# A gated recurrence whose projections take seven block products for eight (one Trainium2 core)

## The chip, the cores and the metric

The kernel runs on one core of a Trainium2 chip. The metric is the device time of one execution in microseconds (us); of several executions the median is taken. The engines have short names: PE (TensorE, matrix products), DVE (VectorE), ACT (ScalarE), POOL (GpSimd) and SP (SyncE, which here only issues DMAs). Each takes its instructions strictly in the order in which they were laid, and waits at an instruction until what it needs is there.

## The reference

A decoder trunk of two layers on 1024 tokens of width 1024, in float32. Layer 0 mixes tokens by a gated linear recurrence (HGRN2), layer 1 by sliding-window attention; each is followed by a gated convolution FFN of width 2816. The change touches the mixer of layer 0:

```python
def hgrn2_mixer(h, w_in, lower_bound, g_norm_w, w_out):
    q, f, i, g = jnp.split(h @ w_in, 4, axis=-1)          # 8 heads of 128 each
    lb = lower_bound.reshape(HG_HEADS, HG_DIM)
    fg = lb + (1.0 - lb) * jax.nn.sigmoid(heads(f))
    o = hgrn2_chunkwise(jax.nn.silu(heads(q)), 1.0 - fg, heads(i), jnp.log(fg))
    o = o * lax.rsqrt(jnp.mean(jnp.square(o), -1, keepdims=True) + RMS_EPS)
    o = o * g_norm_w * jax.nn.silu(heads(g))
    return o.reshape(B, S, D) @ w_out
```

So each head needs four projections of the 1024 x 1024 input x: q (query), f (forget gate), i (values) and g (output gate), each with a 1024 x 128 block of the weights. Then come the recurrence itself, a normalisation by 1/rms, the gate, and the output projection `w_out`.

## The kernel before

Everything is one program on one core, laid by a Python generator. `Order` keeps two clocks while it lays instructions: `od.t`, an estimate of TensorE's time, which every matmul moves on, and `od.v`, an estimate of DVE's. Tasks are generators that say how long to wait on `od.t`; `od.tick`, called after each few matmuls, lays what is due. `od.fill` lays small DVE jobs where DVE's clock is behind. So the order on all engines is written out by hand, and the engines follow it whatever the true times are.

A float32 product is made of three matmuls in a rounded format, "high" times "high", "high" times "low", "low" times "high" (`mm3`, L193 to L197): an operand is split into a rounded copy, written by ACT, and the rest, written by DVE (`low_part`, L166). The input x is turned once, so that features lie on partitions, and lies split in `T`; split weights pass through the twelve places of `HL`, raw weights through three `raw` tiles loaded by SP.

Per head h:

- `qf` (L915) projects f and q, feature-major: 2 halves of 512 tokens x 8 blocks of 128 features x `mm3` each. ACT forms the gate by Sigmoid and two affine steps; q times its sigmoid is formed on DVE (L934).
- `ig_block` (L726) projects i and g token-major: for each of 8 blocks of 128 tokens, 8 pairs of a 512-column and a 256-column matmul (L738, L739). `values` (L698) adds the two halves of the result and forms g times its sigmoid.
- `recur` (L944) is the recurrence of one head: DVE steps by powers of two (`update`), many small matmuls into `psax`, the state `St`, and the output. It is laid into the projections of the next head, so that TensorE has other work while it waits for DVE. `norm` (L1115) multiplies by the gate, takes the squares on ACT (L1122), 1/rms on POOL (L1123, L1124), multiplies by it on DVE (L1126), and turns the head's output into `Y` (for head 7 straight into `T`).

One more job is spread over this stage: the FFN's down-projections take seven products for eight, and the sums of their weight blocks that this needs are made by DMAs from DRAM to DRAM, issued by POOL, half of them adding onto what is there. `weight_sums` (L1188) makes eight such DMAs for each of eight groups, and `sums` (L1199) holds these 64 in the order in which they are laid, two groups interleaved. `slot_begin` (L1181) lays one at the start of each of 60 slots (four of f and q and four of i and g per head), and two in every twelfth. The same POOL queue carries `norm`'s 1/rms.

At the end `moves` (L1164) splits the heads' outputs from `Y` into `T`, and `out_pass` (L1285) begins the output projection while head 7 finishes.

Of the kernel before, what the change touches and what calls it, by code (L numbers as in the profile page):

```python
# [16 lines left out]
P = 128  # L17
# [4 lines left out]
BL = 32  # L22
# [32 lines left out]
class Order:  # L55
# [5 lines left out]
    def __init__(self):  # L61
        self.t = 0.0
        self.v = 0.0
        self.fill = None
        self.chains = []
# [28 lines left out]
    def tick(self):  # L94
        for task in sorted(self.chains, key=lambda k: k[0]):
            if task[0] <= self.t:
                self.step(task)
        while self.fill and self.v < self.t + 1.5 and self.fill():
            pass

    def finish(self, tasks):
        for task in tasks:
            while task[1] is not None:
                self.step(task)


@with_exitstack
def trunk(ctx: ExitStack, tc: tile.TileContext, a: dict, out: bass.AP):
# [20 lines left out]
    Y = cp.tile([P, 8, D], F32, name="Y")  # L129
# [4 lines left out]
    gd = drp.tile([P, NF, S], F32, name="gd")  # L134
    rbd = drp.tile([16, 2 * P], F32, name="rbd")
# [15 lines left out]
    ring = {"hl": 4, "raw": 0}  # L151
# [41 lines left out]
    def mm3(ps, st, mv, start, stop, n=512):  # L193
        nc.tensor.matmul(ps, st(0), mv(0), start=start, stop=False)  # L194
        nc.tensor.matmul(ps, st(0), mv(1), start=False, stop=False)  # L195
        nc.tensor.matmul(ps, st(1), mv(0), start=False, stop=stop)  # L196
# [61 lines left out]
    def turn_block(tb, spread):  # L258
# [5 lines left out]
        split(T[:, 0, :, ts], T[:, 1, :, ts], ps.rearrange("p (k t) -> p k t", k=KC))  # L264

# [411 lines left out]
    with tc.tile_pool(name="t", bufs=1, reuse_waits="tile") as raws, hgrn_pool as hp:  # L677
# [17 lines left out]
        VG = {-1: hp.tile([P, NB, 2, P], F32, name="VG", bufs=2)}  # L695
        values_in, soon, gated = [-1], [], {}

        def values(h, tb, ps):  # L698

            vg = VG[h][:, tb]  # L700
# [4 lines left out]
            if tb == NB - 1:  # L705
                values_in[0] = h
            if tb % 2:
                G = VG[h][:, tb - 1:tb + 1, 1, :]
                sg = hp.tile([P, 2, P], F32, name="sg")
                yield 0.7  # L710
                nc.scalar.activation(sg, G, AF.Sigmoid)
                yield 0.8
                nc.vector.tensor_tensor(G, G, sg, op=ALU.mult)
                od.vec(0.4)

        def first_values(ps):

            pv = ps.rearrange("p (t g c) -> p t g c", t=2, g=2)
            vg = VG[0][:, :2]
            nc.scalar.activation(vg[:, :, 1, :], pv[:, :, 1, :], AF.Sigmoid)  # L720
            nc.scalar.copy(vg[:, :, 0, :], pv[:, :, 0, :])
            yield 1.4
            nc.vector.tensor_tensor(vg[:, :, 1, :], vg[:, :, 1, :], pv[:, :, 1, :], op=ALU.mult)
            od.vec(0.4)

        def ig_block(h, us, tp, ahead=None):  # L726
            if tp == 0:
                VG[h] = hp.tile([P, NB, 2, P], F32, name="VG", bufs=2)
# [5 lines left out]
            for tb in () if ahead else (2 * tp, 2 * tp + 1):  # L734
# [7 lines left out]
                soon.append(od.spawn(values(h, tb, ps)))  # L742
# [50 lines left out]

# [872 lines left out]
```

## Time and profile before

| | us |
|---|---|
| median of 3 runs | 2130.45 (2129.08 to 2130.46) |
| the profiled execution | 2131.54 |
| its span, first to last instruction | 2129.5 |
| TensorE busy | 2118.2 |
| DVE busy | 1713.2 |
| ACT busy | 927.4 |
| POOL busy | 182.2 |

A page of the profile gives the busy time of each engine, the span in 40 slices of 53 us, and the costliest groups of instructions. Other views of the same trace list instructions in order of time, group them by line, or say what an engine was waiting for ("<-issue" where the wait was for nothing that the profile shows, such as a semaphore). In a list by time the columns are start, duration, engine, line, operation, output <- input, count, and in brackets the idle time before it and what ended it. In a list by groups they are busy us, mean ns of one, and idle time before. A matmul's duration is longer than its share of the engine, since matmuls overlap; from start to start is what one costs. The recurrence stage lasts from the start to about 460 us.

### The profile page before, as it was taken

What the parts mean: (1) busy time and instruction counts of PE and PEld (TensorE: products, weight loads), DVE (VectorE), ACT (ScalarE), POOL (GpSimd) and SP (SyncE); (2) the same over time, 40 slices, a digit from 0 to 9 for tenths busy, and PEclk for the clock granted to TensorE, in tenths of its full rate; (3) what the DMA queues carried; (4) which work ended last, traced back from release to release, by engine and by line L of the source; (5) the groups of instructions that cost most, each with busy time, mean ns of one, the idle gap of its engine ahead of it and who ended that gap; (6) DMA issues with size and microseconds to landing.
All of it is one profiled execution on the core that took longest, in us unless ns stands there. A gap on an engine that the chain in (4) does not pass through costs nothing.

```text
span 2129.5 us, 31998 instructions
## 1 busy us (share of the span) xinstructions
PE 2118.2 (99%) x12639; PEld 1777.5 (83%) x12639; DVE 1713.2 (80%) x2322; ACT 927.4 (44%) x1491; POOL 182.2 (9%) x214
## 2 busy tenths in 40 slices
PE   9999999999999999999999999999999999999998
PEld 8888888888888888888888888888888888888887
DVE  4555555677999998887987758969999999978977
ACT  4444444452444444444433356743544444444430
POOL 2011011110100000000001113321000000000002
PEclk9999999999999999999999999999999999999999
DMA  9376577435223222227854611042233222249662
GB/s 262 89 169 139 144 159 174 104 90 186 101 71 108 89 86 78 84 97 265 295 187 155 172 25 46 24 149 89 80 102 96 90 85 84 84 147 324 229 203 104
DMA packets 237421, 280.53 MB, mean 132 GB/s; under 512 B 30120, under 2 KB 160344, under 8 KB 237016
## 3 DMA queue, kind: packets, MB, share of 16 engines
q1 hardware_dynamic: 220960, 231.96, 33.6%
q0 software_dynamic: 15456, 46.16, 10.3%
q8 instruction: 99, 1.62, 0.3%
q10 hardware_dynamic: 856, 0.37, 0.1%
q14 instruction: 50, 0.41, 0.1%
HBM read 238.58 MB, written 86.01 MB: 152 GB/s over the span
## 4 chain that ended last, share of the span: by engine, by line
PE 97%; DVE 2%; DMA 1%; issue 0%; SPq 0%; ACT 0%; DVEq 0%; ACTq 0%
PE psmm L194 17%; PE psmm L196 17%; PE psmm L195 17%; PE psax L194 10%; PE psax L196 10%; PE psax L195 10%; PE psmm L738 5%; PE psax L200 4%; PE psmm L739 3%; PE psmm L200 1%; PE psmm L204 1%; PE psax L1440 1%; PE psax L204 1%; PE psmm L1287 1%; DMA rx<-in_ffn_w_in_dram 0%
## 5 line engine op out<-in xcount | busy, mean ns | idle before, releaser
L194 PE MATMUL psmm<-T,HL 128*128 128x512 f32 x768 | 303.7, 395 | 0.0
L196 PE MATMUL psmm<-T,HL 128*128 128x512 f32 x768 | 299.4, 390 | 0.0
L195 PE MATMUL psmm<-T,HL 128*128 128x512 f32 x768 | 299.1, 389 | 0.0
L498 DVE SCALAR_TENSOR_TENSOR Y<-Y,cwt 128x1023 f32<-128x1023 f32 (+1 forms) x176 | 224.8, 1280 | 44.4 <-ACT Y L496 42.9
L221 ACT CAST HL<-rx 128x1024 fp32r<-128x1024 f32 (+1 forms) x151 | 150.7, 1007 | 174.4 <-PE psmm L195 31.6
L169 DVE TENSOR_TENSOR HL<-rx,HL 128x1024 fp32r<-128x1024 f32 (+1 forms) x151 | 178.5, 1188 | 17.6 <-ACT HL L221 17.2
L738 PE MATMUL psmm<-HL,T 128*128 128x512 f32 x496 | 176.3, 399 | 0.0
L196 PEld LDWEIGHTS psmm<-T,HL 128*128 128x128 f32 x768 | 144.2, 188 | 30.8
L194 PEld LDWEIGHTS psmm<-T,HL 128*128 128x128 f32 x768 | 144.2, 188 | 29.4 <-issue 0.4
L195 PEld LDWEIGHTS psmm<-T,HL 128*128 128x128 f32 x768 | 144.3, 188 | 28.5
L243 POOL TENSOR_TENSOR rs<-rs,nhalf 128x1 f32<-128x1 f32 x32 | 45.0, 1406 | 1287.8 <-DVE rs L242 1287.8
L496 ACT ACTIVATE Y<-Y,cwt 128x1024 f32<-128x1024 f32 x88 | 108.7, 1238 | 102.2 <-DVE Y L485 89.6
L739 PE MATMUL psmm<-HL,T 128*128 128x256 f32 x496 | 138.6, 279 | 0.0
L194 PE MATMUL psax<-T,HL 128*128 128x512 f32 x352 | 137.3, 390 | 0.0
L196 PE MATMUL psax<-T,HL 128*128 128x512 f32 x352 | 137.0, 389 | 0.0
L195 PE MATMUL psax<-T,HL 128*128 128x512 f32 x352 | 137.0, 389 | 0.0
L738 PEld LDWEIGHTS psmm<-HL,T 128*128 128x128 f32 x496 | 93.1, 188 | 21.3
L739 PEld LDWEIGHTS psmm<-HL,T 128*128 128x128 f32 x496 | 93.5, 189 | 0.4
L221 ACT CAST HT<-rx 128x1024 fp32r<-128x1024 f32 (+1 forms) x37 | 35.5, 961 | 124.3 <-DVE rx L452 74.9
L169 DVE TENSOR_TENSOR HL<-raw,HL 128x1024 fp32r<-128x1024 f32 x51 | 62.2, 1221 | 28.0 <-ACT HL L176 27.3
L194 PEld LDWEIGHTS psax<-T,HL 128*128 128x128 f32 x352 | 66.2, 188 | 13.6
L196 PEld LDWEIGHTS psax<-T,HL 128*128 128x128 f32 x352 | 66.0, 187 | 13.7
(316 smaller groups left out, 5225.5 us busy)
## 6 DMA issues: line engine op xcount, KB each, us to landing
rx<-in_ffn_w_in_dram SPq DMA_DIRECT2D x136, 256.0 KB, 3.2
rx<-gd SPq DMA_DIRECT2D x118, 256.0 KB, 3.8
bsd<-in_ffn_w_out_dram POOLq DMA_DIRECT2D x36, 768.0 KB, 8.1
gd<-Y SPq DMA_DIRECT2D x44, 512.0 KB, 2.6
rx<-in_ffn_w_out_dram SPq DMA_DIRECT2D x54, 256.0 KB, 4.5
R<-bsd SPq DMA_DIRECT2D x44, 256.0 KB, 5.1
Y<-in_ffn_w_in_dram SPq DMA_DIRECT2D x40, 256.0 KB, 3.0
bsd<-bsd POOLq DMA_DIRECT2D x12, 768.0 KB, 9.0
```

Of the source, the lines that this page charges most:

```text
L169: make = lambda e: e.tensor_tensor(lo, src, hi.bitcast(F32), op=ALU.subtract)
L194: nc.tensor.matmul(ps, st(0), mv(0), start=start, stop=False)
L195: nc.tensor.matmul(ps, st(0), mv(1), start=False, stop=False)
L196: nc.tensor.matmul(ps, st(1), mv(0), start=False, stop=stop)
L200: nc.tensor.matmul(ps, lhsT, rhs, start=start, stop=stop, **kw)
L204: nc.tensor.transpose(ps, src, ident)
L221: nc.scalar.copy(hi, src)
L243: nc.gpsimd.tensor_tensor(rs, rs, nhalf, op=ALU.pow)
L496: nc.scalar.activation(c, u, AF.Identity, bias=cwt[:, l, 3, ci:ci + 1], scale=cwt[:, l, 2, ci:ci + 1])
L498: nc.vector.scalar_tensor_tensor(c[:, sh:], u[:, :S - sh], cwt[:, l, 2 - sh, ci:ci + 1], c[:, sh:], op0=ALU.mult, op1=ALU.add)
L738: nc.tensor.matmul(ps, T[:, 0, kc, ts], w[:, :, kc % 4, :], start=kc == 0, stop=False)
L739: nc.tensor.matmul(ps[:, :256], T[:, 1, kc, ts], w[:, 0, kc % 4, :], start=False, stop=kc == KC - 1)
```

## The change

For heads 1 to 7 the four projections become two pairs, (f, q) and (g, i), each a product of x with 256 columns of weights. Each pair is taken as a 2 x 2 block product by a scheme with seven block products for eight (Winograd's form): tokens in halves, features in halves, the two projections as the two column blocks. Head 0 is projected as before.

- Sums of x: `sums_of_x` and `last_sums` form four sums of blocks of x once, on DVE, and split them into `TXs` (in `Y`'s two halves and `HL[8:12]`) and into the second half of `T`.
- Sums of weights: for each pair, four sums on DVE in the raw tiles (`job_next`, jobs "a" and "b"), and a split of each of the seven weight blocks (a cast of 512 columns on ACT by `cast_next`, a low part of 512 on DVE), in eight places of `HL`.
- Products: `product(n)` runs 4 x `mm3` of 512 columns. Products 6, 7, 4 and 3 add onto the PSUM bank that holds the sum so far, which `evacuate` has copied out in the meantime, so that partial sums stay in PSUM. Two additions from PSUM per pair go through DVE for products 7 and 3 and one for product 2; the rest are copies on ACT.
- The gates: Silu directly for q and g, Tanh of half the argument for f, on feature-major tiles.
- The values come out feature-major, and are turned back by eight transposes and a copy in `recur`; the output gate is applied after the transposes of `norm`, feature-major. Heads 0 to 5 go through DRAM (`hod`) and come back in `stage` and `move` at the end.
- The 64 DMAs of `sums` are interleaved by four groups, and `product` lays one at the start of each product as long as any is left. There are 98 products, 14 per head.

```diff
-        sums = [one for i in range(0, 8, 2) for two in zip(*groups[i:i + 2]) for one in two]
+        sums = [one for i in range(0, 8, 4) for four in zip(*groups[i:i + 4]) for one in four]
+        SEQ = (1, 2, 6, 5, 7, 3, 4)
+        pairs = [(h, g) for h in range(1, NH) for g in range(2)]
+        line = [(m, p) for m in range(len(pairs)) for p in SEQ]
+        for m in range(len(pairs) - 2):
+            line[7 * m + 6], line[7 * m + 7] = line[7 * m + 7], line[7 * m + 6]
...
+        def job_next(force=False):
...
+                r1, r2 = raw_of[m, 0], raw_of[m, 1]
+                b11, b21, b12, b22 = r1[:, :512], r1[:, 512:], r2[:, :512], r2[:, 512:]
+                if p == "a":
+                    tt(b12, b22, b12, op=sub)
+                    tt(b11, b12, b11, op=add)
+                else:
+                    tt(b21, b21, b11, op=sub)
+                    tt(b11, b22, b11, op=sub)
...
+                w = home(place_of[m, p])
+                low_part(w[:, 1], source(m, p), w[:, 0], None)
+                if p == 4:
+                    pair_load(m + 1, 1)
+                    pair_load(m + 2, 0)
...
+        def evacuate(m, p, ps, taken):
...
+            if p == 1:
+                nc.scalar.copy(first[:, early], ps)
+            elif p == 6:
+                nc.scalar.copy(second[:, early], ps)
+            elif p == 5:
+                nc.scalar.copy(second[:, late], ps)
+            elif p == 4 and g:
+                nc.scalar.copy(first[:, late], ps)
+                values_in[0] = h
+            elif p == 4:
+                forget(h, first, kp, late, ps)
+            else:
+                half, to = {2: (early, first), 7: (late, second), 3: (early, second)}[p]
+                tt(to[:, half], to[:, half], ps, op=add)
+                taken.append(1)
+                yield od.behind(0.1, 0.8)
+                if p != 2:
+                    nc.scalar.activation(to[:, half], to[:, half], AF.Silu)
+                elif g == 0:
+                    forget(h, first, kp, half, to[:, half])
...
+        def product(n):
+            m, p = line[n]
+            ensure(min(n + 2, len(line) - 1))
+            if sums:
+                sums.pop(0)()
+            b = {2: 1, 5: 2, 3: 2}.get(p, 3 * (m % 2))
+            ps = banks[b]
...
+            w = home(n)
+            for k in range(4):
+                mm3(ps, lambda j: w[:, j, k * P:(k + 1) * P], lambda j: moving[p](j, k), k == 0 and p in (1, 2, 5), k == 3, onto=p in (6, 7, 3, 4))
+                od.tick()
...
         def recur(h, qs, fg, kp):
...
-            V, G = VG[h][:, :, 0, :], VG[h][:, :, 1, :]
+            V = VG[h][:, 0, :].rearrange("p (c d) -> p c d", c=NB)
+            if h:
+                ps = psax()
+                for c in range(NB):
+                    tr(ps[:, c * P:(c + 1) * P], V[:, c, :])
+                nc.scalar.copy(VG[h][:, 0, :], ps)
+                yield 1.3
...
         def norm(h, pv):
...
-            nc.vector.tensor_tensor(og, og, ss.unsqueeze(2).to_broadcast([P, NB, P]), op=ALU.mult)
+            nc.vector.tensor_tensor(og, og if h == 0 else pv, ss.unsqueeze(2).to_broadcast([P, NB, P]), op=ALU.mult)
...
+                nc.vector.scalar_tensor_tensor(G, ps, par[:, 16:17], G, op0=ALU.mult, op1=ALU.mult)
...
+            if h < NH - 2:
+                nc.sync.dma_start(hod[h], G)
...
+            for tp in range(2, 4):
+                ig_block(0, us, tp)
+            opened[0] = len(line)
+            firsts = od.spawn(last_sums(0), 0.2)
+            soon_all()
+            banks = [psmm() for _ in range(4)]
+            lead, moved = 1, []
+            for n, (m, p) in enumerate(line):
+                if m == 0 and p == 5:
+                    od.finish([firsts])
+                product(n)
+                h, g = pairs[m]
...
+                elif n > lead and line[n - lead][1] == 4 and pairs[line[n - lead][0]][1] == 0 and n - lead < 90:
+                    mr = line[n - lead][0]
+                    od.finish(evacs[mr])
+                    ready.append((pairs[mr][0], targets[mr]))
```

A head is `ready`, and its recurrence can begin, one product after the last product of its f and q.

More of the change, by code (lines that the diff above doesn't have):

```diff
@@ L134, in trunk @@
     gd = drp.tile([P, NF, S], F32, name="gd")
+    hod = [drp.tile([P, S], F32, name=f"hod{h}") for h in range(NH - 2)]
     rbd = drp.tile([16, 2 * P], F32, name="rbd")
@@ L1037, in recur @@
             update(1)
-            early = stash(2, idle[:, :S])
+            early = stash(2, VG[h - 1][:, 0, :] if h else hp.tile([P, S], F32, name="og"))
             yield od.behind(0.0, 0.5)
```

474 lines of the change are left out of this document (290 added, 184 removed).

## Prediction

> **What bounds the kernel now.** I read the page first (busy shares), then the stretch of one head by engine, then the weights of single matmuls, then GpSimd's instructions in order of time, because the change moves work onto that queue's clock.
>
> ```profile
> span 2129.5 us, 31998 instructions
> PE 2118.2 (99%) x12639; PEld 1777.5 (83%) x12639; DVE 1713.2 (80%) x2322; ACT 927.4 (44%) x1491; POOL 182.2 (9%) x214
> q0 software_dynamic: 15456, 46.16, 10.3%
> 234.68:290.73 56.05, 56.05 (x569) 47.90 (x572) 32.06 (x60) 24.74 (x55) 5.71 (x7) 1.00 0.53 127
> 17.40:70.00 52.60, 52.60 (x272) 44.77 (x271) 25.48 (x39) 22.76 (x36) 6.16 (x8) 1.00 0.89 225
> ```
>
> TensorE is busy 99% of the span. The fourth line is one period of the recurrence (from one head's column sums to the next head's): 56.05 us, with columns PE, weight loads, DVE, ACT, POOL, granted clock, DMA share, GB/s. PE never rests, DVE is busy 32.06 us (57%). The clock is at 1.00. So in this stage time is PE work, as long as nobody else is late. The last line is the start of the stage.
>
> ```profile
> 164.75 0.40 PE L738 MATMUL psmm<-HL,T 128*128 128x512 f32 x1
> ...
> 171.34 0.39 PE L738 MATMUL psmm<-HL,T 128*128 128x512 f32 x1
> 171.69 0.39 PE L194 MATMUL psmm<-T,HL 128*128 128x512 f32 x1
> ...
> 176.49 0.39 PE L194 MATMUL psmm<-T,HL 128*128 128x512 f32 x1
> 217.41 0.87 PE psax L204 x8
> ```
>
> Durations overlap, so I use starts. Between the two L738 lie 19 pairs of L738 and L739: 6.59 / 19 = 0.347 us a pair. Between the two L194 lie 21 matmuls of 512 columns: 4.80 / 21 = 0.229 us each. Eight transposes (a line of the chain of waits) take 0.87 us.
>
> **The change on TensorE.** Before, a head has 96 matmuls for f and q (2 halves x 8 blocks x 2 x 3), 96 x 0.229 = 22.0 us, and 64 pairs for i and g, 64 x 0.347 = 22.2 us. After, each of the two pairs is 7 products x 4 blocks x 3 = 84 matmuls, 19.2 us. Saved: 2.8 + 3.0 = 5.8 us a head. Added: eight transposes to turn the values back, 0.87. Net 4.9 us a head, 34 us for heads 1 to 7, all of it on the path. A period becomes 56.05 - 4.9 = 51.2 us, and as it holds 14 products, one product with its share of the recurrence takes 3.66 us.
>
> **On DVE and ACT.** These rows are DVE's groups in the same period:
>
> ```profile
> L169 DVE TENSOR_TENSOR HL<-raw,HL 128x1024 fp32r<-128x1024 f32 x4 | 4.9, 1220 | 0.4 <-ACT HL L176 0.4
> L703 DVE TENSOR_TENSOR VG<-VG,psmm 128x256 f32<-128x256 f32 x8 | 3.3, 416 | 5.4 <-ACT VG L701 5.4
> L713 DVE TENSOR_TENSOR VG<-VG,sg 128x256 f32<-128x256 f32 x4 | 1.7, 422 | 1.0 <-ACT sg L711 1.0
> L934 DVE TENSOR_TENSOR qs<-qs,psmm 128x512 f32<-128x512 f32 x2 | 1.4, 686 | 4.2 <-ACT qs L931 4.2
> L1016 DVE TENSOR_TENSOR kp<-kp,tot 128x512 f32<-128x512 f32 x6 | 4.1, 683 | 0.0
> ```
> ```profile
> 17.57 1.28 ACT L854 ACT_TABLE_LOAD   x1
> 61.25 1.23 DVE L1025 TENSOR_TENSOR St<-qs,kp 128x1024 f32<-128x1024 f32 x1
> ```
>
> The first four go (11.3 us). In their place a head gets 14 low parts, 8 sums of weights and 6 additions from PSUM, 28 operations of 512 elements at 0.683 (the fifth row) = 19.1 us. The gate multiplies after the transposes instead of before, at the same size. DVE: 32.06 - 11.3 + 19.1 = 39.9 us of 51.2, 78%. It fits, with less room: each product asks for the weights two products ahead, some 5 us, and the longest run of recurrence instructions laid in one piece (L1025 to L1034: two of 1024 elements at 1.23 and six of 512) is 6.6. I bound stalls from this at 0 and 3 us a head (two such misses) and take 0 in the sum, since the wait found below covers heads 1 to 4. ACT's 24.74 us grow by at most 14 casts, 11 copies or silus and the values' copy, 26 at some 0.7 (DVE's row, the nearest), before what goes is taken off: 43 of 51.2. Should Tanh and Silu need a table load (1.28, seen once at the start) at each change between them, four a head, it is 48: still under the period, so nothing in the sum. At the start, 16 sums of x and 16 low parts, 32 x 0.683 = 21.9 us, come on top of 25.48 in 52.60: 90%. A stall there is 0 to 8 us; I take 0 for the same reason. At the end the values' transposes and a copy stand in head 7's chain, 0 to 3 us, taken as 0. The staging of heads 0 to 5 through DRAM is on SP, whose queue before only waits for free raw tiles; landing late, it falls into the same 3.
>
> **On POOL.** The sums of w_out (L1188 to L1199) are 64 GpSimd DMAs, 32 of them accumulating (L1194). No data ties them to TensorE; only their place among GpSimd's other instructions does. Before, `slot_begin` lays one or two in each of 60 slots, 8 or 9 a head. After, `product` lays one in each of the first 64 products: 14 a head. Between them, in the same in-order queue, stands each head's 1/rms (L1123, L1124), and DVE's next step (L1126) waits for it. This is a stretch before, from one head's 1/rms to the next:
>
> ```profile
> 266.55 1.66 POOL L1124 TENSOR_TENSOR ss<-ss,nhalf 128x8 f32<-128x8 f32 x1
> 268.17 0.68 POOL L1193 DMA_DIRECT2D bsd<-in_ffn_w_out_dram  x1
> 274.04 1.00 POOL L1194 DMA_DIRECT2D bsd<-in_ffn_w_out_dram  x1 [5.19 <-issue]
> 281.52 0.97 POOL L1194 DMA_DIRECT2D bsd<-in_ffn_w_out_dram  x1 [6.48 <-issue]
> 290.78 0.96 POOL L1194 DMA_DIRECT2D bsd<-in_ffn_w_out_dram  x1 [8.29 <-issue]
> 298.90 0.96 POOL L1194 DMA_DIRECT2D bsd<-in_ffn_w_out_dram  x1 [7.16 <-issue]
> 299.50 1.40 POOL L1193 DMA_DIRECT2D bsd<-bsd  x2
> 309.45 0.98 POOL L1194 DMA_DIRECT2D bsd<-in_ffn_w_out_dram  x1 [8.55 <-DMA bsd<-bsd]
> 318.54 0.99 POOL L1194 DMA_DIRECT2D bsd<-in_ffn_w_out_dram  x1 [8.11 <-issue]
> 322.32 0.19 POOL L1123 TENSOR_SCALAR ss<-ss 128x8 f32<-128x8 f32 x1 [2.79 <-ACT sq L1122]
> ```
>
> Look at the starts: an accumulating sum starts 7.5 to 9.3 us after the one before, mean of the first three steps 8.3. The wait is marked "issue": no semaphore held it. Its median landing (below) is 7.9, so I read this as: the next one cannot go out until the last has landed. Nine sums filled 50.4 us, and the 1/rms came in only 2.79 us early. Fourteen will not fit into 51.2.
>
> ```profile
> bsd<-in_ffn_w_out_dram POOLq DMA_DIRECT2D x28, 768.0 KB, 7.9
> 347.42 1.20 POOL L1193 DMA_DIRECT2D bsd<-in_ffn_w_out_dram  x2 [6.69 <-issue]
> 354.15 1.15 POOL L1193 DMA_DIRECT2D bsd<-in_ffn_w_out_dram  x2 [5.53 <-issue]
> 9.10 1.22 POOL L1193 DMA_DIRECT2D bsd<-in_ffn_w_out_dram  x2
> 55.88 1.40 POOL L1193 DMA_DIRECT2D bsd<-bsd  x2
> 103.99 0.19 POOL L1123 TENSOR_SCALAR ss<-ss 128x8 f32<-128x8 f32 x1 [46.71 <-ACT sq L1122]
> 439.56 1.01 POOL L1194 DMA_DIRECT2D bsd<-in_ffn_w_out_dram  x1 [2.64 <-DMA bsd<-bsd]
> ```
> ```profile
> POOL ss L1123 <- ACT sq L1122: 128.9, 7, 46.7
> DVE og L1126 <- POOL ss L1124: 0.8, 1, 0.8
> ```
>
> Prices: an accumulating sum 8.0 us (every fourth is a smaller one, so a little under 8.3); a plain one from the weights 3.4 (two per 6.73); four copies bsd to bsd 4 us (two made the next step 10.55 instead of 8.3, rows 298.90 and 309.45).
>
> Places: head 0's recurrence began at 61.25 (L1025, above) and its 1/rms ran at 103.99, 42.7 us later, with GpSimd idle for it since 57. After, two blocks of i and g (32 pairs, 11.1 us) come behind head 0's f and q, so its 1/rms is due at 93, and product 0 starts at about 63. Some 8 products lie before it, with the 8 plain sums: these are free. Head h begins after product 14(h-1)+8, its 1/rms is due 42.7 / 3.66 = 12 products later, so head 1's stands behind sum 20 and head 4's behind sum 62. Due times: 63 + 21 x 3.66 = 140 and 63 + 63 x 3.66 = 294.
>
> Arrivals: from 95, head 1's comes behind 8 accumulating sums, 4 copies and the issue of one more, 64 + 4 = 68 us: 163, late by 23. Head 4's comes behind 31 accumulating (248), four lots of copies (16), 8 plain (27), less the last landing (8), plus three 1/rms (6): 95 + 289 = 384, late by 90. What stands behind it: DVE's L1126, behind that the low parts and additions that TensorE needs. TensorE runs on for the planned 5.4 us less 1.9 of L1123/L1124, and two products of stock: 11 us. It stalls 79 us in all, spread over heads 1 to 4; once the sums are out the gain per head is real again.
>
> **Sum.** 2131.5 us (this execution, span 2129.5 and 2.0 around it) - 34 + 79 = 2176; the median of the runs shown lies 1.1 lower, so **2175**. Bounds of the unknown: over the whole stage, from 9.10 to 439.56, the 63 sums took 430 us less 128.9 of waiting for ACT (the waits view) and 13 for seven 1/rms, 288 in all, 4.6 each; with landings that ran on during those waits this is too low a price, and I take 4.3 as the end. Then 55 sums take 237 us, head 4's arrives at 338, late by 44, and the stall is 33: 2130. If accumulating sums take 8.5 (31 x 0.5 more, copies 5) the stall is 100, and with 8 us of start and end 2204. The case's own range is 2130 to 2204.
>
> **What the Trainium skill says against it.** Its page "DMA: Bandwidth & Descriptors", section "Anatomy of one DMA — SWDGE (gpsimd) path", fits such a transfer as 2.0 us plus bytes / 436 GB/s, an estimate of 3.8 us for 768 KB; the trace has 7.9. By that rule 14 sums take 53 us, nearly a period, and the time would be near the first rival's. The measurement decides the sum.
>
> **Rivals.** (1) *Not slower: sums overlap.* The change interleaves four groups instead of two, so neighbours never depend on each other; if "issue" hides a dependence, several fly at once. From the page's q0 row all 64 use 10.3% of 2129.5 us = 219 us of all engines, 3.4 each: 55 take 187 us, head 4's 1/rms arrives at 95 + 187 + 6 = 288, not late. Then -34 + 5 of small stalls: 2101. It decides from about 3.6 us a sum. For it: DMA share is 0.53 in the quoted period. Against: rows 274.04 to 298.90, neighbours without a dependence, 8 us apart. (2) *DVE's in-order queue binds*, sums or not: 3 us x 7 stalls, 2131 - 34 + 21 - 1 = 2117. For it 78%; against, that the idle time in DVE's rows (5.4 and 4.2 us) is waiting for work to come, so it was spare.
>
> **Chances.** Forecast 0.66 (0.62 of it slower by over 0.2%, the rest near no change), rival 1 0.25, rival 2 0.09. A measurement tells about 0.2% (4 us) from no change. Slower 0.62, same 0.05, faster 0.33. For 8 in 10 the range reaches down to rival 1: 2100 to 2204.
>
> **What would show it.** Right: what L1126 becomes waits tens of us for POOL's ss in heads 1 to 4 (0.8 us in seven heads before, the waits row above), ss no longer waits for ACT there, some of PE's slices 3 to 8 fall below 9, and after the 64th product heads take 51 us. A product's matmuls start 0.229 us apart throughout. Wrong: accumulating sums that start under 4 us apart, or ss that still waits for ACT.

## The result, and the profile after

| | before | after |
|---|---|---|
| median of 4 executions, us | 2130.45 (2129.08 to 2133.24) | 2227.64 (2225.69 to 2231.68) |
| ratio after / before | | 1.0457, 95% interval 1.0439 to 1.0475 |
| profiled span, us | 2129.5 | 2226.6 |
| span less PE busy, us | 11.3 | 110.0 |

The kernel became slower by 97 us where 45 were forecast. The sign and the mechanism named for it are there, but as the 34 us of matmuls were saved, 131 us were lost, and only 45.5 of them are stalls of the kind that the forecast priced, at 79. Here are PE's slices and granted clock on the page of the kernel before, and the same rows with the busy times after:

```profile
PE   9999999999999999999999999999999999999998
...
PEclk9999999999999999999999999999999999999999
```
```profile
span 2226.6 us, 31496 instructions
...
PE 2116.6 (95%) x12303; PEld 1759.3 (79%) x12303; DVE 1779.9 (80%) x2422; ACT 970.7 (44%) x1562; POOL 185.0 (8%) x214
...
PE   8796978799999999999999999999999999999998
...
PEclk9898988899999999999999999999999999999999
```

Read the PE row first. Before, PE was busy for 2118.2 us; with the forecast's 34 us of matmuls gone it should be 2084.2. It is 2116.6. So some 32 us are not work, but work done slowly, and the clock row says where: it is below 9 in five of the first ten slices, and before it was 9 throughout. On top of that, PE is idle 98.7 us longer than before. The bookkeeping of the 97.1 us of span is then: 98.7 of idle time + 32.4 of slow matmuls - 34 of matmuls saved.

GpSimd's queue in order of time, at the 1/rms (ss) of head 0, of head 1 and of head 4 (start, duration, engine, line, operation; in brackets the idle time before it):

```profile
128.25 0.73 POOL L1198 TENSOR_SCALAR ss<-ss 128x8 f32<-128x8 f32 x1 [76.65 <-ACT sq L1197]
129.07 2.13 POOL L1199 TENSOR_TENSOR ss<-ss,nhalf 128x8 f32<-128x8 f32 x1
131.18 1.03 POOL L1226 DMA_DIRECT2D bsd<-in_ffn_w_out_dram  x1
...
207.82 0.88 POOL L1226 DMA_DIRECT2D bsd<-in_ffn_w_out_dram  x1 [6.49 <-issue]
208.38 0.83 POOL L1225 DMA_DIRECT2D bsd<-bsd  x1
209.29 0.19 POOL L1198 TENSOR_SCALAR ss<-ss 128x8 f32<-128x8 f32 x1
...
409.72 0.88 POOL L1226 DMA_DIRECT2D bsd<-in_ffn_w_out_dram  x1 [7.42 <-issue]
410.68 0.19 POOL L1198 TENSOR_SCALAR ss<-ss 128x8 f32<-128x8 f32 x1
410.96 1.66 POOL L1199 TENSOR_TENSOR ss<-ss,nhalf 128x8 f32<-128x8 f32 x1
```

Head 1's and head 4's ss stand directly behind a sum, with no wait for ACT: their data had been there. From the end of head 0's 1/rms (131.2) to head 4's ss GpSimd took 279.5 us; the forecast had 95 to 384, 289. But the chain began at 131 and not at 95, and before it began GpSimd had stood idle for 76.65 us. The waits of the stage (total, times, longest):

```profile
POOL ss L1198 <- ACT sq L1197: 176.6, 3, 76.7
...
DVE og L1201 <- POOL ss L1199: 55.4, 4, 22.9
...
PE psax L228 <- DVE og L1201: 33.2, 2, 19.5
...
PE psmm L218 <- DVE VG L1358: 12.3, 1, 12.3
```

L1201 is what L1126 became: 55.4 us of waiting for GpSimd, where before it was 0.8. PE's share of this is the last two rows, three stalls of 45.5 us in all (L1358 of the last row stands in DVE's queue behind head 4's L1201). That leaves 53 us of the new idle time, and the slow matmuls, for which the forecast's sum had no term. Of the eleven other stalls of over 2 us up to 640 us, six end on a copy of a partial sum, like this one at the third product (PE in order of time):

```profile
84.46 0.80 PE L218 MATMUL psmm<-Y,HL 128*128 128x512 f32 x1 [5.66 <-ACT fg L1346]
85.06 0.63 PE L219 MATMUL psmm<-Y,HL 128*128 128x512 f32 x1
85.48 0.63 PE L220 MATMUL psmm<-Y,HL 128*128 128x512 f32 x1
85.91 0.63 PE L218 MATMUL psmm<-Y,HL 128*128 128x512 f32 x1
```

L1346 is ACT's copy of a partial sum out of PSUM: the next product may not add to that bank before. And the matmuls behind the stall start 0.43 us apart, where it was 0.229 before.

The last place is behind the stage. The first pass of the output projection, found by its line, before and then after (first and last start are the two numbers ahead of the tile shape):

```profile
L1287 PE MATMUL psmm<-HL,T x84: 387/389/499, 459.1 to 485.2; 128*128 128x512 f32 x84
```
```profile
L1493 PE MATMUL psmm<-HL,T x84: 388/389/501, 538.1 to 563.1; 128*128 128x512 f32 x84
```

From its start to the end of the span it was 1670.4 us and is 1688.5. Followed along GpSimd's chain, this execution differs from the forecast by 36 us at the chain's start, -9 in it, 7 from head 4's ss to this pass (127.4, where 459.1 + 45 - 384 = 120 were forecast), and 18 behind: 52 more than the forecast 2176, against 2228.4.

### The profile page after: what moved, and what is told of

Same layout as the page of the kernel before. It is cut to its first block, busy times and chain, and to the rows that moved or that the text cites. A ratio compares the mean times of both kernels' runs of the same rounds, so it can differ in the third digit from the quotient of the medians.

```text
span 2226.6 us, 31496 instructions
## 1 busy us (share of the span) xinstructions
PE 2116.6 (95%) x12303; PEld 1759.3 (79%) x12303; DVE 1779.9 (80%) x2422; ACT 970.7 (44%) x1562; POOL 185.0 (8%) x214
## 4 chain that ended last, share of the span: by engine, by line
PE 78%; issue 10%; DVE 5%; DMA 3%; POOL 2%; ACT 2%; SPq 0%; DVEq 0%; POOLq 0%; ACTq 0%
PE psmm L218 15%; PE psmm L220 15%; PE psmm L219 14%; PE psax L218 9%; PE psax L220 9%; PE psax L219 9%; DMA bsd<-bsd 2%; PE psax L224 2%; PE psmm L228 1%; PE psmm L224 1%; PE psax L1642 1%; POOL bsd L1226 1%; PE psax L228 1%; PE psmm L1493 1%; DVE HL L193 0%
## 5 line engine op out<-in xcount | busy, mean ns | idle before, releaser
L218 PE MATMUL psmm<-T,HL 128*128 128x512 f32 x768 | 307.6, 401 | 17.8 <-DVE VG L1358 12.3
L220 PE MATMUL psmm<-T,HL 128*128 128x512 f32 x768 | 302.0, 393 | 3.0 <-DVE HL L193 3.0
L219 PE MATMUL psmm<-T,HL 128*128 128x512 f32 x768 | 301.8, 393 | 0.0
L523 DVE SCALAR_TENSOR_TENSOR Y<-Y,cwt,Y 128x1023 f32<-128x1023 f32 (+1 forms) x176 | 225.2, 1281 | 45.5 <-ACT Y L521 43.9
L218 PEld LDWEIGHTS psmm<-T,HL 128*128 128x128 f32 x768 | 146.5, 191 | 48.2 <-DVE VG L1358 12.7
L220 PEld LDWEIGHTS psmm<-T,HL 128*128 128x128 f32 x768 | 145.5, 189 | 35.2 <-DVE HL L193 4.2
L219 PEld LDWEIGHTS psmm<-T,HL 128*128 128x128 f32 x768 | 146.3, 191 | 29.2 <-DVE T L193 0.5
L193 DVE TENSOR_TENSOR HL<-raw,HL 128x512 fp32r<-128x512 f32 (+1 forms) x121 | 93.1, 788 | 31.5 <-ACT HL L1271 18.6
L218 PE MATMUL psmm<-HL 128*128 128x512 f32 x220 | 88.2, 401 | 8.6 <-ACT qs L1348 7.3
L1271 ACT CAST HL<-raw 128x512 fp32r<-128x512 f32 x98 | 55.2, 619 | 91.8 <-DVE raw L1291 62.8
L220 PE MATMUL psmm<-HL 128*128 128x512 f32 x220 | 87.1, 396 | 0.0
L219 PE MATMUL psmm<-HL 128*128 128x512 f32 x220 | 87.1, 396 | 0.0
```

Source lines behind the costliest of these rows:

```text
L193: make = lambda e: e.tensor_tensor(lo, src, hi.bitcast(F32), op=ALU.subtract)
L218: nc.tensor.matmul(ps, st(0), mv(0), start=start, stop=False, skip_group_check=onto)
L219: nc.tensor.matmul(ps, st(0), mv(1), start=False, stop=False, skip_group_check=onto)
L220: nc.tensor.matmul(ps, st(1), mv(0), start=False, stop=stop, skip_group_check=onto)
L523: nc.vector.scalar_tensor_tensor(c[:, sh:], u[:, :S - sh], cwt[:, l, 2 - sh, ci:ci + 1], c[:, sh:], op0=ALU.mult, op1=ALU.add)
L1271: nc.scalar.copy(home(n)[:, 0], source(m, p))
```

## Experiments

Nineteen rows, with idle time (span less PE busy) and slow matmuls (PE busy less 2084.2; for a kernel of the old form less 2118.2). "Base" says what was edited. Idle and slow are those of the profiled execution, which lies up to 5 us from the median, in e17_room 9 above it. The runs of one kernel spread over 2 to 8 us, over 10 in e17_room and 17 in e2_recip_dve, so a gain of 6 us between two medians says little.

| run | base | median us | ratio to before, 95% | idle | slow |
|---|---|---|---|---|---|
| after | | 2227.64 | 1.0457 (1.0439 to 1.0475) | 110.0 | 32.4 |
| e1_spread | after | 2180.62 | 1.0238 (1.0221 to 1.0256) | 67.6 | 23.6 |
| e2_recip_dve | after | 2192.61 | 1.0280 (1.0247 to 1.0314) | 78.2 | 30.3 |
| e3_before_crowd | before | 2170.68 | 1.0189 (1.0174 to 1.0204) | 41.9 | 4.9 |
| e4_casts_late | after | 2230.70 | 1.0472 (1.0453 to 1.0490) | 113.2 | 33.9 |
| e5_rotate | e1 | 2165.78 | 1.0168 (1.0153 to 1.0184) | 59.1 | 20.1 |
| e6_dve_light | e1 | 2174.25 | 1.0204 (1.0187 to 1.0221) | 64.9 | 24.0 |
| e7_casts_late2 | e1 | 2188.16 | 1.0273 (1.0258 to 1.0289) | 74.0 | 27.1 |
| e8_forget | e1 | 2169.18 | 1.0187 (1.0171 to 1.0202) | 64.6 | 21.4 |
| e9_moves | e8 | 2172.74 | 1.0195 (1.0180 to 1.0210) | 61.1 | 25.6 |
| e11_no_xsum | e8 | 2179.83 | 1.0225 (1.0208 to 1.0242) | 70.6 | 25.5 |
| e12_before_tail | before | 2133.70 | 1.0019 (1.0009 to 1.0028) | 12.1 | 1.2 |
| e13_dve_reads | e8 | 2186.28 | 1.0264 (1.0247 to 1.0281) | 76.8 | 26.7 |
| e14_rx_first | e8 | 2170.19 | 1.0181 (1.0163 to 1.0199) | 60.4 | 18.7 |
| e15_after_rx | after | 2230.78 | 1.0461 (1.0441 to 1.0481) | 112.3 | 35.2 |
| e16_ahead | e8 | 2159.09 | 1.0136 (1.0119 to 1.0153) | 59.0 | 13.9 |
| e17_room | e8 | 2161.82 | 1.0156 (1.0135 to 1.0176) | 62.2 | 21.9 |
| e18_ahead4 | e8 | 2191.72 | 1.0285 (1.0268 to 1.0302) | 82.7 | 27.6 |
| e19_ahead_room_rx | e8 | 2167.99 | 1.0179 (1.0163 to 1.0194) | 58.0 | 23.9 |

### GpSimd's queue: is it the place of the sums?

Three ways to move the one against the other: spread the same 64 sums over all 98 products; take the 1/rms off GpSimd (a plain reciprocal on VectorE in its place); and crowd the sums in the kernel before.

```diff
-            if sums:
+            while sums and 64 - len(sums) < 8 + (n + 1) * 57 // 98:
                 sums.pop(0)()
```

> The changed kernel, with eight sums laid at product 0 and the other 56 spread evenly over the 98 products, 8 per head. Crowding theory (the 14 sums per head in GpSimd's queue hold up the 1/rms of heads 1 to 4, some 81 us): about 2147 us, between 2135 and 2160; head 4's 1/rms waits for ACT again, and a head takes 52 to 53 us throughout. Rival (the stalls come from the order on ACT and DVE, and GpSimd's waits are a symptom): less than 20 us gained, 2208 or more.

```diff
-            nc.gpsimd.tensor_scalar(ss, ss, 1.0 / P, RMS_EPS, op0=ALU.mult, op1=ALU.add)
-            nc.gpsimd.tensor_tensor(ss, ss, nhalf.to_broadcast([P, NB]), op=ALU.pow)
             yield 5.4
+            nc.vector.tensor_scalar(ss, ss, 1.0 / P, RMS_EPS, op0=ALU.mult, op1=ALU.add)
+            nc.vector.reciprocal(ss, ss)
```

> The changed kernel with its crowded sums as they are, but the norm's factor made on DVE, as a reciprocal in place of the power -1/2 on GpSimd; so nothing of the recurrence stands in GpSimd's queue. The output is not the reference's, since the square root is left out. Queue theory: the place in the queue is what costs, so this gains as much as spreading, about 2147 us (2135 to 2165). Rival (the crowded DMAs themselves take the bandwidth from the weight loads): it stays above 2208.

```diff
         def slot_begin():
...
-            for _ in range(2 if n % 12 == 11 else 1):
+            for _ in range(1 if n % 4 == 3 else 2):
```

> The kernel before, with its sums laid as crowded as in the change: 14 per head instead of 8 or 9, nothing else. Queue theory: heads 1 to 3 find their 1/rms late by about 20, 38 and 54 us in all; less 10 us of stock and with some us of slow clock about 2175 us (2160 to 2190). Rival (crowding only hurts beside the new products): within 5 us of 2130.

The crowded kernel before came out as expected: 2170.68, and its waits name the same step, GpSimd's ss and then PE behind DVE:

```profile
DVE og L1126 <- POOL ss L1124: 47.8, 4, 18.7
...
PE psax L204 <- DVE og L1126: 32.4, 3, 14.1
```

So crowding the sums alone, without the rest of the change, costs 40 us. In e1_spread ss waits for ACT again in all eight heads and no stall of PE ends behind ss, and yet the gain is 47 us and not 80:

```profile
POOL ss L1198 <- ACT sq L1197: 191.9, 8, 54.8
```

47 is about what the three stalls of the kernel after added up to (45.5). With GpSimd out of the way 50 us over the kernel before remain. e2_recip_dve gains 35, less than the queue theory wanted and more than its rival allowed, although no 1/rms stands behind a sum. Here are the stretch 97 to 230 us by engine of e2_recip_dve and of e1_spread (columns as in the prediction; the last three are clock, DMA share, GB/s):

```profile
97.00:230.00 133.00, 113.92 (x1048) 93.12 (x1047) 80.80 (x148) 57.17 (x125) 20.14 (x28) 0.93 0.81 189
```
```profile
97.00:230.00 133.00, 121.46 (x1131) 99.45 (x1132) 85.24 (x151) 65.17 (x137) 17.86 (x21) 0.97 0.61 141
```

and the wait for the projections' own weights, in e2_recip_dve and in e1_spread:

```profile
DVE raw L1290 <- DMA raw<-in_hgrn_w_in_dram: 35.3, 6, 13.8
```
```profile
DVE raw L1290 <- DMA raw<-in_hgrn_w_in_dram: 22.7, 7, 7.2
```

Crowded sums fill the DMA engines to 0.81 in place of 0.61, and DVE waits 12.6 us longer for the weights. This points to a second cost of the sums, by bandwidth, of the size of the 12 us between the two medians. That it is the cause was not shown, and one of e2_recip_dve's four runs took 2178.09, as little as e1_spread.

### What remains: whose queue holds up PE?

e1_spread holds one undisturbed period and one that is typical, by engine:

```profile
270.60:321.80 51.20, 51.18 (x516) 42.60 (x516) 34.91 (x61) 25.16 (x54) 6.88 (x8) 1.00 0.46 125
321.80:381.30 59.50, 54.26 (x521) 44.79 (x517) 39.96 (x73) 28.89 (x62) 11.17 (x13) 0.94 0.80 171
```

The first is the forecast's 51.2 us to the tenth: the saving of matmuls is real. It is the best of six such periods. The other has 5.2 us of idle PE, and 3.1 us more of busy PE at a clock of 0.94. From head 0's ss to head 4's (its row below) e1_spread needs (353.56 - 127.93) / 4 = 56.4 us a head, more than the 56.05 before.

Where do the losses lie? In the kernel before, head 0's ss ran at 103.99, and by the forecast's place for it, 11.1 us earlier, it was due at 92.9; from there to the first pass of the output projection (459.1 before) a kernel that saves 34 us and loses nothing takes 332.2 (459.1 - 34 - 92.9). The kernel after loses 35 us ahead of head 0's ss, 78 from there to the pass and 18 behind. For e1_spread (ss at 127.93, pass from 486.9) it is 35, 27 and 18. So moving the sums took 51 us, all from the middle, and left the start and the end as they were.

The first stall in e1_spread that ends on a copy, in order of time:

```profile
81.65 0.69 DVE L1294 TENSOR_TENSOR raw<-raw,raw 128x512 f32<-128x512 f32 x1
82.37 0.62 ACT L1271 CAST HL<-raw 128x512 fp32r<-128x512 f32 x1 [4.96 <-DVE raw L1294]
82.90 0.61 ACT L845 CAST T<-VG 128x512 fp32r<-128x512 f32 x1
...
83.42 0.58 ACT L1346 COPY fg<-psmm 128x512 f32<-128x512 f32 x1
...
84.05 0.79 PE L218 MATMUL psmm<-Y,HL 128*128 128x512 f32 x1 [5.68 <-ACT fg L1346]
```

PE waits for ACT's copy of a partial sum; that stands behind a cast, which waits for DVE's sum of weights, which stands behind the recurrence. Theory A: it is the reading of the banks by ACT. Theory B: DVE is late as a whole. Five edits on e1_spread or e8_forget were to tell them apart. e4_casts_late, made earlier on the kernel after, had tried the casts while GpSimd still bound:

> The changed kernel, with the casts of weights on ACT laid only when the planner's clock has the sums they read done; sums crowded as they are. Order theory (ACT stands behind DVE's weight sums, 92 us of waits in the trace, and everything behind it is late): 20 to 40 us gained, 2187 to 2208. Crowding theory: those waits are mostly time in which GpSimd is waited for, so less than 10 us, 2218 or more.

It gained nothing (2230.70), as the theory of the queue wanted. The five:

```diff
 # e5_rotate
-            b = {2: 1, 5: 2, 3: 2}.get(p, 3 * (m % 2))
+            b = n % 4
...
-                mm3(..., k == 0 and p in (1, 2, 5), k == 3, onto=p in (6, 7, 3, 4))
+                mm3(..., k == 0, k == 3)
 # e6_dve_light
-                low_part(w[:, 1], source(m, p), w[:, 0], None)
+                low_part(w[:, 1, :64], source(m, p)[:, :64], w[:, 0, :64], None)
 # e7_casts_late2 (the edit of e4_casts_late)
+            need = {6: "a", 7: "a", 5: "b", 4: "b"}.get(p)
+            if not force and need and od.t < summed_at.get((m, need), 0.0):
+                return False
...
 # e8_forget
                 elif g == 0:
+                    yield 4.0
                     forget(h, first, kp, half, to[:, half])
 # e13_dve_reads, for products 1, 6 and 5
-                nc.scalar.copy(first[:, early], ps)
+                nc.vector.tensor_copy(first[:, early], ps)
```

> e1_spread with the four PSUM banks used in turn by all products, each started afresh: no product adds to a bank that ScalarE or VectorE must read first. The partial sums are left out, so the projections lack their earlier parts; instructions and their number stay. Theory A (TensorE waits for the reading of a partial sum, which stands in ScalarE's in-order queue behind recurrence copies and casts): the idle times of TensorE in e1_spread that end on the copies L1346, L1348, L1350 (5.7 + 4.6 + 2.3 + 4.2 + 3.6 = 20 us) go, and with them most of the half-speed matmuls behind them (some 2 us each): 2180 falls to about 2150. Theory B (VectorE's queue is late as a whole, and the bank is only where it shows): the idle times come back at the weights' low parts or the recurrence; 2170 or more.

> e1_spread with each weight's low part written for 64 of its 512 columns only (the rest of the low halves is left out); every instruction, its place and its waits stay, VectorE has some 0.5 us x 14 = 7 us a head less to do. Theory B (VectorE's load stretches everything): a head's recurrence, 58 us from its first product to its 1/rms in e1_spread against 48 before, goes back towards 50, TensorE's idle times at the start and once per head shrink, the tail comes earlier: 2130 to 2150. Theory A alone (ScalarE's queue holds the reading of the banks): few of them change, 2165 or more.

> e1_spread with a cast of summed weights laid into ScalarE's queue only once the plan has VectorE's sums done (what gained nothing while GpSimd's queue bound). If the casts that wait for VectorE's sums hold up the reading of the partial sums: the 5.7 us at 78 us and the waits of HL L1271 for raw (29.7 + 28.8 us) shrink, 2180 to about 2165. If the recurrence's copies and the forget gate's activations are what stands ahead: 2176 to 2184.

> e1_spread with the three activations of the early half's forget gate laid 4 us later in the plan, so that the next copy of a partial sum stands ahead of them in ScalarE's queue. Theory A: the idle times of 4.6, 4.2 and 3.6 us that end on L1350 at 217, 329 and 387 us fall by the 2.2 us of those activations or go, with the half-speed matmuls behind them: 2180 to 2160. Theory B: 2176 to 2184.

> e8_forget with the copies of partial sums out of PSUM (those of the first, third and fourth product of each seven) on VectorE in place of ScalarE; the places in the plan stay as they were. Theory A (ScalarE's in-order queue holds these readings): the 5.7 us at 79 us and the 2 to 3 us once per head that end on such a copy fall to 1 us or less, with the half-speed matmuls behind them, while VectorE has some 4 us more a head: 2169 to 2150 or 2158. Theory B (any engine is as late): 2166 to 2175, with the same idle times now ending on VectorE.

Without any adding to a read bank (e5_rotate) 15 us go, half of what A expected: no product waits for a bank now, but the stall at the fourth product, 5.5 us in e1_spread, has grown, and it ends on one of ACT's casts, that of an input sum:

```profile
91.23 0.80 PE L218 MATMUL psmm<-T,HL 128*128 128x512 f32 x1 [8.97 <-ACT T L845]
```

DVE with a sixth less to do (e6_dve_light) gains 6, where B wanted 30 to 50: theory B is out as a matter of load. Casts laid later lose 8. The gate's activations laid later, so that the copy comes first, gain 11, a half of what A wanted. With the copies on DVE, the same places in the plan and ACT relieved (e13_dve_reads), 17 us are lost, and the stalls now end on DVE:

```profile
PE psmm L218 <- DVE VG L1348: 19.2, 6, 6.1
...
PE psmm L218 <- DVE fg L1346: 6.1, 1, 6.1
```

So the readings of partial sums are a part, some 15 us by e5_rotate. That the rest has no one engine for its cause is argued from these runs, not shown. One more, at the start: the last input sum, which overwrites input that head 0's values have just used, left out.

```diff
-            firsts = od.spawn(last_sums(0), 0.2)
+            firsts = od.spawn(iter(()))
```

> e8_forget with the last sum of the input, which overwrites blocks of the input that head 0's values have just used, left out (the products that use it read the input's own blocks). Theory (at the start a product waits for this sum's casts, which stand in ScalarE's queue behind head 0's recurrence): the idle time of 5.5 us at 91 us goes with the half-speed matmuls behind it, head 0's recurrence, 69 us before, gets 6 to 9 us shorter: 2169 to about 2161. If the next late thing takes its place: 2166 to 2172.

At the place it did what was expected (the stall at 91 us fell from 5.5 to 2.0 us, and head 0's ss came 5 us earlier), and in sum it lost 11 us: the plan, which lays everything by its own two clocks, came out differently later on, with stalls in other places. This is a limit of all these edits: each also shifts the order that is laid after it, by an estimated 10 us in either direction (the sizes of e7_casts_late2 and e11_no_xsum), and the 15 us of e5_rotate are not much more.

The last theory was that the weights come too late and the readings are only where it shows:

```diff
 # e16_ahead (e18_ahead4: n + 4)
-            ensure(min(n + 2, len(line) - 1))
+            ensure(min(n + 3, len(line) - 1))
 # e17_room
-            od.fill, od.hook, od.room = lay, hook, 0.5
+            od.fill, od.hook, od.room = lay, hook, 1.5
```

> e8_forget with each product asking for the weights three products ahead instead of two. If TensorE's stalls at the start and once per head come from weights made too late: 2169 falls to 2150 or 2160. If they come from the partial sums read too late, more weights laid ahead of those readings on ScalarE and VectorE make it no better: 2168 to 2180.

> e8_forget with the plan allowed to lay VectorE's weight work 1.5 us ahead of the time planned instead of 0.5 (as the kernel before does). Weights too late: 2155 to 2165. Readings and recurrence steps too late, which then stand behind more weight work: 2170 to 2185.

> e8_forget with weights asked for four products ahead. If the lead is what was short, a fourth product's lead takes away what is left of the stalls once per head: 2159 falls to 2145 or 2155. If three already cover it and what remains is the recurrence's own order, the start's input sums and the end: 2155 to 2165.

> Three products of lead, weight work laid up to 1.0 us ahead, and the buffers of the late weights in the other place: the edits that gained or lost nothing, together. If their gains add: 2148 to 2156. If each new order makes stalls of its own: 2156 to 2168. In neither case below the kernel before (2130).

A third product of lead gains 10 us (2159.09, the best version of the change), 1.5 us of room 7. Of what e16_ahead still loses, 30 us lie ahead of head 0's ss, 11 from there to the pass and 20 behind. A fourth product of lead loses 33 against the third, which neither theory had; where PE waits for ACT's copies of partial sums, which I read as standing behind that much more weight work, the stalls are longest:

```profile
PE psmm L218 <- ACT qs L1350: 29.7, 6, 16.4
```

In e8_forget, with two products of lead, that row was 7.7 us in 3 waits. So both theories seem to hold a part: lead for the weights is paid for by the readings, and of the three leads tried three products is the best. Their gains did not add (e19_ahead_room_rx, 2167.99). No version came below the kernel before.

### What remains: the end

All versions of the change lose 16 to 26 us behind the stage, from the pass's last matmul to the end. Three theories, each with one edit: six staged blocks turned in one piece between steps of head 7's recurrence (e9_moves); head 7's recurrence ending later against the matmuls that cover it (e12_before_tail, in the kernel before); a load into memory that the change keeps in use to the end (e14_rx_first, and the same in the kernel after, e15_after_rx).

```diff
 # e9_moves
+            highs.append((h0, half))
-            yield od.behind(0.0, 0.6 + 0.4 * n)
+            yield od.behind(0.0, 0.6 + 0.4 * n) + 1.6 * (len(highs) - 1)
...
-            od.finish(moved[:7] + [params])
+            od.finish([params])
...
 # e12_before_tail
-        lead = [0, 3, 2, 2, 2, 2, 1, 0]
+        lead = [0, 3, 2, 2, 2, 2, 1, 2]
 # e14_rx_first, e15_after_rx
-            tail["R"] = pool.tile([P, 3, 1024], F32R, name="HT")
             tail["raw"] = [pool.tile([P, 1024], F32, name=f"rx{i}") for i in range(3)]
+            tail["R"] = pool.tile([P, 3, 1024], F32R, name="HT")
```

> e8_forget with the low parts of the values that come back from DRAM laid 1.6 us apart instead of in one piece as soon as the high parts are cast. Theory (the tail's 17 us come from head 7's recurrence, which takes 56 us instead of 45 because VectorE turns six staged blocks, 6.7 us in one piece, between two of its steps): head 7's recurrence gets 4 to 6 us shorter, TensorE's 5.4 us of idle time at the first layer norm shrinks, the time from the last product of out_pass to the end falls by 5 to 10 us: 2169 to about 2161. If something else sets the tail (loads of weights that are issued late, the four matrices of the output projection): 2167 to 2172.

> The kernel before, with the last head's recurrence begun two blocks of i and g (11.1 us of matmuls) later; nothing else differs. Theory (what the change loses behind the stage, 17 us, comes from head 7's recurrence ending some 10 us later against the matmuls that could cover it): the same loss appears here, idle TensorE around the first layer norm and half-speed matmuls behind it: 2130 to 2140 or 2147. If other things set the tail (staged values, loads of the output projection's weights as the change orders them): 2129 to 2133.

> e8_forget with the three buffers for late weights allocated ahead of the ones beside them, so that they lie over the projections' raw tiles and not over the values' tiles; no instruction changes. Theory (the change keeps a values tile in use up to head 7's last instruction, and the third load of the output projection's late weights, whose buffer lies there, holds SyncE's queue for 27.7 us and all loads behind it): that wait goes, the loads are issued by 510 us, TensorE's 5.4 us of idle time at the first layer norm falls by at least half, with the half-speed matmuls behind it: 2169 to 2155 or 2162. If the loads have time enough: 2167 to 2172.

> The changed kernel with the same exchange of buffers and nothing else. As this loss lies behind the stage that GpSimd's queue sets, it should gain what the run on e8_forget gains: 2227 to about 2213 or 2220; by the other theory 2224 to 2230.

None of the three explains it: 2172.74, 2133.70, 2170.19 and 2230.78. The later recurrence of e12_before_tail costs 4 us (2133.70 for 2129.75), a quarter of the loss at most; the other two edits gain nothing. The exchange of buffers is a lesson in reading a wait. In e8_forget SyncE waited 27.7 us for the tile that lay under the load; with the tile elsewhere it waited 31.3 us for the next thing, a VectorE instruction behind head 7's last values (SyncE's waits in e8_forget, then in e14_rx_first):

```profile
SPq L188 <- DVE T L193: 27.9, 2, 27.7
```
```profile
SPq L188 <- DVE TX L193: 31.3, 1, 31.3
```

The idle time itself is plain, 5.4 us ahead of the first layer norm's transposes, here in e8_forget; what sets it stays open.

```profile
559.70 0.69 PE L228 MATMUL psmm<-ident,Y 128*128 128x128 f32 x2 [5.41 <-DVE Y L279]
```

## Why the prediction was wrong, step by step

- **TensorE, -34 us: right.** The undisturbed period of e1_spread is 51.20 us for 51.2, with PE busy for 51.18.
- **A sum's price: right.** GpSimd's chain from head 0's 1/rms to head 4's took 279.5 us for 289. Ten sums had gone out before it, where 8 were forecast, so it held 54 in place of 55. The mechanism (L1201 waits tens of us for ss, ss no longer for ACT in heads 1 to 4) is in the trace, and e1_spread and e3_before_crowd show it as cause, from both sides.
- **"Head 4's due 294 ... late by 90", stall 79: mis-sized.** The stall was 45.5, and moving the sums gave 47. The due time supposed that TensorE runs on at 51.2 us a head. With GpSimd out of the way it reaches that point only at 354, as GpSimd's row in e1_spread shows. Head 4's ss ran at 411, so it was late by 57, and less the forecast's 11 us of stock that is 46, the stalls that were measured. GpSimd's chain and TensorE's delays run side by side, so what TensorE loses by itself comes off GpSimd's stall.

```profile
127.93 0.73 POOL L1198 TENSOR_SCALAR ss<-ss 128x8 f32<-128x8 f32 x1 [54.76 <-ACT sq L1197]
...
353.56 0.39 POOL L1198 TENSOR_SCALAR ss<-ss 128x8 f32<-128x8 f32 x1 [0.87 <-ACT sq L1197]
```

- **"A stall there is 0 to 8 us; I take 0", since the later wait covers it: this step failed most.** The start lost 35 us: head 0's ss ran at 128.25 for the 93 that were due. The recurrence of head 0 began 9 us late (its first DVE step at 58.77; 61.25 less the 11.1 is 50.2), and it took 69.5 us in place of 42.7, with 14.7 us of idle PE from 68 to 131 us and a clock of 0.89. All this lies ahead of head 0's 1/rms, for which GpSimd stood idle. Which of the start's waits is worth how much was not shown. A delay ahead of the chain that binds is not covered by it; it starts the chain later. Eight sums before it were free in the forecast for just this reason.
- **"0 and 3 us a head, and take 0": failed, hidden in the result.** In the kernel after most of it lies beside GpSimd's chain. In e1_spread it shows: 2180.6, where 2130.45 - 34 = 2096.5 would be the kernel without stalls. The second rival named this (DVE's in-order queue binds, sums or not) and priced it at 3 us for 7 stalls, 21 us; it is 84, with the start and the end, and not DVE's queue alone. The loads had been forecast well: DVE is busy 39.06 us in a mean period of e1_spread, for 39.9, and ACT 28.45, for at most 43. The price was a stall's length. Missing were the number of places (a product can now wait for a bank, for its weights or for an input sum) and the slow matmuls.
- **The wait that partial sums in PSUM add was not counted at all.** The description of the change says that a bank is added to after it has been copied out; the prediction priced the copies as ACT's time, and not as something PE waits for. e5_rotate puts it at some 15 us.
- **The end, "0 to 3 us, taken as 0": failed, 18 us**, with the cause open.
- **The granted clock had no term.** 32 us of the result are lost by matmuls that run at about half speed behind stalls. "A product's matmuls start 0.229 us apart throughout" is refuted by the rows at 84.46.
- **The range.** Its upper end, 2204, put 8 us on the start and the end, against 53 measured. The errors also ran against each other: a stall taken 33 us too long hid part of what had been taken as 0, so that the result lies only 24 us above the range. The first rival (sums overlap) did not occur: in the kernel after no accumulating sum starts less than 6.35 us after the one before.

## What to carry to other kernels

Where two in-order chains meet, cost the wait from the later start, not only from the length: a delay ahead of the chain that binds adds in full, one beside it is absorbed. When a change splits work into more dependent pieces, list what each piece waits for (a buffer read, an operand made, an input rewritten) and price each kind; average busy shares (DVE at 78%) say little about them. And a hand-written order that fitted the old durations may have to be planned anew for the new ones: here the saving of 34 us was real, 131 us of idle and slow TensorE ate it, and the lead of the weights alone moved the time from 2159 to 2192.

## What the runs showed of the hardware

**The price of a stall does not follow its length.** Behind most stalls the matmuls start 0.43 us apart for some microseconds. Here are, by engine, the seven microseconds behind a stall of 14.1 us in e3_before_crowd, and then in the kernel after behind stalls of 19.5, 2.20 and 2.18 us (the clock is the third number from the end):

```profile
177.35:184.35 7.00, 7.00 (x31) 6.32 (x32) 6.45 (x10) 0.56 (x2) 1.22 (x2) 0.67 0.92 256
```
```profile
212.55:219.55 7.00, 7.00 (x47) 5.70 (x51) 6.93 (x11) 2.15 (x4) 1.52 (x2) 0.76 1.13 388
492.04:499.04 7.00, 7.00 (x55) 5.53 (x56) 0.93 (x3) 4.20 (x6) 0.00 (x0) 0.76 0.46 150
70.94:77.94 7.00, 7.00 (x171) 5.53 (x172) 4.57 (x9) 2.36 (x4) 0.00 (x0) 1.00 0.02 5
```

The clock is 0.76 behind 2.20 us as it is behind 19.5, and 1.00 behind 2.18. The kernel after has 14 stalls of over 2 us in its first 640 us; behind the other eleven it is 0.56 to 0.79, lowest behind one of 4.24 and one of 12.3 us. Seven microseconds at these clocks lose an estimated 27 us in all, 2 us a stall, most of the 32.4 by which PE is slow. By PE's busy time, e3_before_crowd pays 4.9 us for three stalls, 1.6 each. So a stall of some 2 us can cost nearly twice its length, and one of 19.5 hardly more than its length. The Trainium skill, page "TensorE: Matmul & The Clock Gate", section "HAM oscillation — how this bites in real kernels", advises to leave no idle gap over about 3.4 us; here a gap of 2.20 us was followed by a clock of 0.76, so that keeping gaps under that length was not enough.

**GpSimd's accumulating DMAs go out one at a time.** Where nothing else lies between two of them, they start 6.35 to 11.66 us apart in the kernel after, 8.4 in the median, and the wait is marked as one for nothing that the profile shows ("issue"). In e1_spread one waited 13.42 us; the DMA engines (the last number but one of the lines by engine) were busy to 0.73 in that step, and to 1.00 in one of 8.01 us, so how full they were does not explain it:

```profile
139.74 0.96 POOL L1226 DMA_DIRECT2D bsd<-in_ffn_w_out_dram  x1 [7.84 <-issue]
147.75 0.88 POOL L1226 DMA_DIRECT2D bsd<-in_ffn_w_out_dram  x1 [7.05 <-issue]
...
172.85 0.97 POOL L1226 DMA_DIRECT2D bsd<-in_ffn_w_out_dram  x1 [13.42 <-issue]
```
```profile
139.74:147.75 8.01, 6.83 (x49) 4.91 (x51) 6.14 (x11) 3.55 (x6) 0.96 (x2) 1.00 1.00 217
158.44:172.85 14.41, 11.95 (x88) 9.61 (x86) 6.89 (x14) 7.79 (x15) 1.00 (x1) 1.00 0.73 172
```
